# Hybrid state-space and linear-attention trunk: coefficient loads three tiles ahead, output-map signs on the powers, norm scale on the last projection's weights

## The chip, the cores and the metric

The kernel runs on one core of a Trainium2 chip. The metric is device microseconds of that core, the median of the timed runs shown. The profile is of one further execution, taken by the hardware profiler.

## The reference

Two layers act on one sequence of 512 positions with 1024 channels, all in float32. Each layer is `x <- x + RMSNorm(mixer(RMSNorm(x)))`. Cut to what matters here:

```python
def s5_layer(u, lam_re, lam_im, log_dt, b_re, b_im, c_re, c_im, d):
    lam = lax.complex(lam_re, lam_im)
    lam_bar = jnp.exp(lam * jnp.exp(log_dt)[:, None])
    b_bar = ((lam_bar - 1.0) / lam)[..., None] * lax.complex(b_re, b_im)
    bu = jnp.einsum('gnp,blgp->blgn', b_bar, u)
    _, states = lax.associative_scan(combine, (a, bu), axis=1)   # s_t = lam_bar s_{t-1} + bu_t
    y = jnp.einsum('gpn,blgn->blgp', lax.complex(c_re, c_im), states).real
    return y + d * u

def gla_branch(p, w_gate_up, b_gate, norm_g):
    q, k, v, r, lr = jnp.split(p, ...)
    g = jax.nn.log_sigmoid(lr @ w_gate_up + b_gate) / 16
    o = gla_chunked(heads(q) * 256 ** -0.5, heads(k), heads(v), heads(g))   # 4 heads, 64 positions a chunk
    return rms_norm(o, norm_g).reshape(1, 512, 2048) * jax.nn.silu(r)

# layer 0: p = u @ ev_w_in; ya = gelu(s5_layer(a_in)); ya = ya * sigmoid(ya @ w_glu + b) * silu(a_z)
#          yb = conformer_conv(b_val, b_gate: causal depthwise convolution, 31 taps) * silu(b_z)
#          y = concat([ya, yb]) @ ev_w_out
# layer 1: y = gla_branch(u @ od_w_in, ...) @ od_w_out
```

The state-space layer has 64 groups of 16 channels, each with a complex state of 64. The scale `norm_g` of the head norm in layer 1 has 512 entries, the same for each of the 4 heads.

## The kernel before, in words

**Projections.** A float32 product is made of three TensorE products of rounded halves: high by high, high by low, low by high (`mm_st` L181, `mm_mv` L792). All weights come in one list of 0.5 MB blocks of 128 x 1024 in the order of use. `w_raw` (L113) issues a block's load on SyncE's queue into one of three buffers `wraw` (L118). `w_split` (L134) makes the high half `wh` by a ScalarE cast (L143, two buffers) and the low half `wl` (three buffers): for blocks 0 to 47 and 56 to 63 by a negated ScalarE copy (L130) and an accumulating DMA that GpSimd issues (L131), for the others by a VectorE subtraction (L149). A few blocks, the last four of the list among them, go into buffers of their own (`wres`, `hres`, `lres`).

**State space.** The channels are worked in eight tiles of 128 (c = 0 to 7). `s5_params` (L308) computes the powers of the state's factor, `pr` (real and imaginary, 64 groups x 9 powers) and `prb` (the powers times the input map). `s5_prep(c)` (L513) loads tile c's coefficients `cb` (256 KB: both parts of the output map, both parts of the input map; L519, two buffers), and ScalarE makes two signed copies: `csp` (real part, sign by partition half, L522, which is also the stationary side of a matmul at L551) and `ci` (minus the imaginary part, L523, one buffer). For each half of the tile's groups an outer product of `prb` and the input map gives `bmt` (L528, L530, L532, on VectorE for c = 0 and 1, on GpSimd after), TensorE transposes it (L544), ScalarE copies that to `bm` (L546); TensorE multiplies `csp` by `bmt` (L551), ScalarE copies the result out to `ks` (L554), TensorE transposes `ks` (L555) and VectorE adds it into `kt` (L557). An outer product of `pr` with `csp` and `ci` on VectorE gives `cme` (lines L528, L530 and L532 again, the product with `ci` in the tile `pt`). GpSimd makes phase tables `ph` (L507 to L509) for each pair of tiles, which SyncE copies to `ct` and `st` (L573).

**Convolution.** h (L680) is a gated product, followed by 31 multiply-adds a tile on VectorE (L655), low in priority.

**Linear attention.** `gate(h)` (L965) takes the projection of head h, ScalarE applies SiLU (L970), and GpSimd multiplies by the norm scale, broadcast to all partitions in `ng` (L939, 128 x 512): L971, four times a head. VectorE scales the head's attention output by its inverse root mean square and this gate (L1129). The result is split into `oth` and `otl` and multiplied by the blocks of `w_out1`: eight for heads 0 and 1, in the course of head 2, and eight for heads 2 and 3 at the end, in `proj_tail` (L872; matmuls L800 to L802 and, for the last four blocks, L894 to L898).

**What sets the order.** The Tile framework orders each engine's instructions by simulating a timeline (`schedule_with_timeline_sim=True`), with priorities: `feed()` raises, `background()` lowers. Each engine then runs its own list strictly in order, and a waiting instruction holds everything behind it on that engine. DMAs stand in the list of the engine that issues them, mostly SyncE.

Of the kernel before, what the change touches and what calls it, by code (L numbers as in the profile page):

```python
# [9 lines left out]
F32 = mybir.dt.float32  # L10
F32R = mybir.dt.float32r
# [6 lines left out]
P = 128  # L18
# [33 lines left out]
def trunk(ctx: ExitStack, tc: tile.TileContext, A: dict, out: bass.AP, dbg: dict | None = None):  # L52
# [50 lines left out]
    for h in range(HEADS):  # L103
        wv, wr = ([A["w_vr"][o + h, j] for j in range(4)] for o in (0, 4))
        wqk = [A["w_qk"][2 * h + j] for j in range(2)] + [A["w_qk"][8 + 2 * h + j] for j in range(2)]
        wlist.extend(wv + wr + wqk if h == 0 else wqk + wv + wr)
        if h >= 2:
            for n in range(2):
                for j in range(4):
                    wlist.append(A["w_out1"][n, (h - 2) * 4 + j])  # L110
    wst = {"next_raw": 0, "next_split": 0, "raw": {}, "hl": {}, "low": {}}

    def w_raw():  # L113
        i = wst["next_raw"]
        if i >= len(wlist):
            return
        raw = wpool.tile([P, 1024], F32, tag="wraw", bufs=3, name=f"wraw{i}")
        SY.dma_start(raw, wlist[i])  # L118
        wst["raw"][i] = raw
        wst["next_raw"] = i + 1  # L120
# [13 lines left out]
    def w_split(dst=None):  # L134
# [6 lines left out]
        h = wpool.tile([P, 1024], F32R, tag="wh", bufs=2, name=f"wh{i}") if dst is None else dst[0]  # L141
        with feed():
            SC.copy(h, raw)  # L143
# [12 lines left out]
    def feed():  # L156
        return tc.high_priority(offset=1500)
# [150 lines left out]
    def s5_params():  # L308
# [148 lines left out]

        G.memset(md, 0.0)
# [53 lines left out]

    def s5_prep(c):  # L513
# [4 lines left out]
        cb = h5.tile([P, 4, GC, GP], F32, tag="cb", bufs=2, name=f"cb{c}")  # L518
        SY.dma_start(cb, A["s5cb"][c])  # L519
        cr_ = csps[c % 2]  # L520
        ci_ = h5.tile([P, GC, GP], F32, tag="ci", bufs=1, name=f"ci{c}")
        SC.activation(cr_[:, :, 0:GP], cb[:, 0], AF.Copy, scale=sgn)  # L522
        SC.mul(ci_, cb[:, 1], -1.0)  # L523
# [13 lines left out]
        for h in range(2):  # L537
# [22 lines left out]
            outer(V, cme[:, hs], pt2, h, pr, cr_[:, hs, 0:GP], ci_[:, hs], 3)  # L560
            yield
        kd = kt_d[c % 2]
# [136 lines left out]

    for c in range(2):  # L700
        run(s5_prep(c), 5)
# [236 lines left out]
    ng = pa.tile([P, S], F32, name="ng")  # L938
    SY.dma_start(ng, A["gla_g"].partition_broadcast(P))  # L939
# [25 lines left out]
    def gate(h):  # L965
        accs = proj_mv(u1h, u1l)
        rg = []
        for tt in range(TT):
            r_ = sbt_((P, S), F32, f"rg{h}{tt}")
            SC.activation(r_, accs[tt], AF.Silu)  # L970
            G.tensor_tensor(out=r_, in0=r_, in1=ng, op=ALU.mult)  # L971
            rg.append(r_)
        return rg
# [247 lines left out]
```

## Time and profile before

| | |
|---|---|
| Timed runs | 941.74, 946.74, 941.3 us; median 941.74 |
| Profiled execution, its own time | 946.76 us |
| its span (first to last instruction) | 945.0 us |
| mean granted TensorE clock | 0.983 |
| TensorE matmuls busy | 899.4 us (95%) |
| VectorE busy | 640.9 us (68%) |
| ScalarE busy | 482.6 us (51%) |
| GpSimd busy | 249.1 us (26%) |

The profiled execution took 1.76 us beyond its span. In rows of a timeline the first number is the start in us from the span's start, the second the duration in us, then engine, line and operation, the output tile, `<-`, the inputs and the shapes. In brackets at the end is how long the engine had been idle before, and what released it. SPq is SyncE's queue: a row there is the issue of a DMA, not its transfer, and its duration with xN includes the waits between N issues. Line numbers are those of the kernel before.

### The profile page before, as it was taken

What the parts mean: (1) busy time and instruction counts of PE and PEld (TensorE: products, weight loads), DVE (VectorE), ACT (ScalarE), POOL (GpSimd) and SP (SyncE); (2) the same over time, 40 slices, a digit from 0 to 9 for tenths busy, and PEclk for the clock granted to TensorE, in tenths of its full rate; (3) what the DMA queues carried; (4) which work ended last, traced back from release to release, by engine and by line L of the source; (5) the groups of instructions that cost most, each with busy time, mean ns of one, the idle gap of its engine ahead of it and who ended that gap; (6) DMA issues with size and microseconds to landing.
All of it is one profiled execution on the core that took longest, in us unless ns stands there. A gap on an engine that the chain in (4) does not pass through costs nothing.

```text
span 945.0 us, 12129 instructions
## 1 busy us (share of the span) xinstructions
PE 899.4 (95%) x4396; PEld 720.8 (76%) x4396; DVE 640.9 (68%) x1206; ACT 482.6 (51%) x691; POOL 249.1 (26%) x258
## 2 busy tenths in 40 slices
PE   5995998999999999999998979999999999999996
PEld 4873776777777887778887768888888888888875
DVE  7952999999989989832568546695384232744646
ACT  6542785876678855564444555343543242523430
POOL 2793656563123422011045002010200020000222
PEclk9998999999999999999999989999999999999998
DMA  9978887788988885289454112202222224324412
GB/s 272 252 184 203 222 203 183 179 194 204 216 219 229 205 235 183 86 223 204 154 193 139 49 58 98 84 29 90 89 76 80 75 82 136 133 89 164 192 45 89
DMA packets 54955, 142.74 MB, mean 151 GB/s; under 512 B 14256, under 2 KB 15792, under 8 KB 54896
## 3 DMA queue, kind: packets, MB, share of 16 engines
q1 hardware_dynamic: 46832, 112.62, 36.0%
q0 software_dynamic: 8064, 29.36, 17.2%
q8 instruction: 34, 0.56, 0.2%
q14 instruction: 25, 0.20, 0.1%
HBM read 95.18 MB, written 13.22 MB: 115 GB/s over the span
## 4 chain that ended last, share of the span: by engine, by line
PE 69%; DVE 12%; ACT 3%; DMA 3%; issue 1%; POOL 0%; DVEq 0%; ACTq 0%
PE ps_mm L186 10%; PE ps_mm L187 10%; PE ps_mm L189 10%; PE ps_mm L802 10%; PE ps_mm L800 9%; PE ps_mm L801 9%; DVE ps_cv L655 3%; PE ps_aux L1082 2%; DMA wraw<-in_w_vr_dram 1%; PE ps_aux L628 1%; DVE cme L528 1%; DVE pt L530 1%; DMA wraw<-in_w_out_dram 1%; PE ps_mm L894 1%; PE ps_mm L895 1%
## 5 line engine op out<-in xcount | busy, mean ns | idle before, releaser
L143 ACT CAST wh<-wraw 128x1024 fp32r<-128x1024 f32 x126 | 132.0, 1048 | 160.9 <-PE ps_mm L801 93.2
L149 DVE TENSOR_TENSOR wl<-wraw,wh 128x1024 fp32r<-128x1024 f32 x70 | 86.7, 1240 | 123.0 <-ACT wh L143 123.0
L655 DVE SCALAR_TENSOR_TENSOR ps_cv<-h,cw,ps_cv 128x512 f32<-128x512 f32 x232 | 161.8, 747 | 2.7 <-ACT ps_cv L652 1.8
L186 PE MATMUL ps_mm<-u0h,wh 128*128 128x512 f32 x320 | 128.5, 403 | 0.4 <-DVE u0l L305 0.2
L187 PE MATMUL ps_mm<-u0l,wh 128*128 128x512 f32 x320 | 128.1, 401 | 0.0
L800 PE MATMUL ps_mm<-wh,u1h 128*128 128x512 f32 x240 | 95.9, 401 | 3.5 <-ACT wh L143 3.1
L801 PE MATMUL ps_mm<-wh,u1l 128*128 128x512 f32 x240 | 96.1, 400 | 0.0
L131 POOL DMA_DIRECT2D wl<-wraw x56 | 48.9, 883 | 178.4 <-ACT wl L130 172.6
L802 PE MATMUL ps_mm<-wl,u1h 128*128 128x512 f32 x240 | 93.0, 404 | 1.7 <-DVE wl L149 1.7
L189 PE MATMUL ps_mm<-u0h,wl 128*128 128x512 f32 x320 | 82.7, 396 | 0.9 <-DMA wl<-wraw 0.9
L130 ACT ACTIVATE wl<-wraw 128x1024 fp32r<-128x1024 f32 x56 | 59.2, 1057 | 27.0 <-DMA wraw<-in_w_in_dram 14.0
L186 PEld LDWEIGHTS ps_mm<-u0h,wh 128*128 128x128 f32 x320 | 61.0, 191 | 15.3 <-issue 1.1
L187 PEld LDWEIGHTS ps_mm<-u0l,wh 128*128 128x128 f32 x320 | 61.0, 191 | 13.8 <-issue 1.1
L189 PEld LDWEIGHTS ps_mm<-u0h,wl 128*128 128x128 f32 x320 | 59.3, 188 | 15.1 <-DMA wl<-wraw 1.8
L800 PEld LDWEIGHTS ps_mm<-wh,u1h 128*128 128x128 f32 x240 | 45.8, 191 | 15.0 <-ACT wh L143 3.6
L971 POOL TENSOR_TENSOR rg<-rg,ng 128x512 f32<-128x512 f32 x16 | 24.2, 1542 | 123.6 <-ACT rg L970 123.6
L802 PEld LDWEIGHTS ps_mm<-wl,u1h 128*128 128x128 f32 x240 | 45.9, 192 | 13.3 <-DVE wl L149 2.5
L801 PEld LDWEIGHTS ps_mm<-wh,u1l 128*128 128x128 f32 x240 | 45.9, 191 | 10.6
L187 PE MATMUL ps_mm<-u1l,wh 128*128 128x512 f32 x128 | 50.3, 393 | 0.0
L186 PE MATMUL ps_mm<-u1h,wh 128*128 128x512 f32 x128 | 50.2, 392 | 0.0
L1065 POOL TENSOR_TENSOR kr<-kr,fac 128x384 f32<-128x384 f32 x8 | 9.1, 1133 | 124.5 <-DVE rr L205 65.1
L800 PE MATMUL ps_mm<-wh,oth 128*128 128x512 f32 x96 | 37.8, 396 | 0.6 <-ACT wh L143 0.6
(341 smaller groups left out, 2001.5 us busy)
## 6 DMA issues: line engine op xcount, KB each, us to landing
wl<-wraw POOLq DMA_DIRECT2D x56, 512.0 KB, 5.9
wraw<-in_w_in_dram SPq DMA_DIRECT2D x40, 512.0 KB, 4.9
wraw<-in_w_out_dram SPq DMA_DIRECT2D x32, 512.0 KB, 3.2
wraw<-in_w_vr_dram SPq DMA_DIRECT2D x32, 512.0 KB, 3.2
wraw<-in_w_qk_dram SPq DMA_DIRECT2D x16, 512.0 KB, 3.2
tm<-kt_d SPq DMA_DIRECT2D x8, 512.0 KB, 6.2
wraw<-in_w_glu_dram SPq DMA_DIRECT2D x8, 512.0 KB, 5.6
wraw<-in_w_pw_dram SPq DMA_DIRECT2D x8, 512.0 KB, 4.5
```

What stands on the lines that cost most here:

```text
L130: SC.activation(l, raw, AF.Copy, scale=-1.0)
L131: G.dma_start(l.bitcast(F32), raw, accum_op=ALU.add)
L143: SC.copy(h, raw)
L149: V.tensor_tensor(out=l, in0=raw, in1=h.bitcast(F32), op=ALU.subtract)
L186: PE.matmul(acc, whv[:, k, :], xh[:, k, :], start=(k == 0), stop=False)
L187: PE.matmul(acc, whv[:, k, :], xl[:, k, :], start=False, stop=False)
L189: PE.matmul(acc, wlv[:, k, :], xh[:, k, :], start=False, stop=(k == KT - 1))
L655: V.scalar_tensor_tensor(out=acc, in0=h[:, k:k + S], scalar=cw[:, c, k:k + 1], in1=acc, op0=ALU.mult, op1=ALU.add)
L800: PE.matmul(accs[tt], xh[:, kt, ts_], whj, start=(first and j == 0), stop=False)
L801: PE.matmul(accs[tt], xl[:, kt, ts_], whj, start=False, stop=False)
L802: PE.matmul(accs[tt], xh[:, kt, ts_], wlj, start=False, stop=(last and j == 1))
L971: G.tensor_tensor(out=r_, in0=r_, in1=ng, op=ALU.mult)
```

## The change

Three edits. First, the coefficient tile `cb` gets three buffers, tiles 0 to 2 are loaded before the preparation starts, and tile c + 3 is loaded at the end of tile c's preparation. Second, after `prb` is made, the signs go once onto the powers: `pr`'s real part is multiplied by the sign column, its imaginary part by −1, two VectorE operations of 128 x 576. The outer products for `cme` read `cb` directly, `ci` and its eight ScalarE copies are gone; `csp` stays for the matmul. Third, the norm scale is no longer multiplied into the gates. It is loaded as 4 x 128, transposed on TensorE to a column tile `ngc` of 128 x 4, and applied to the 16 blocks of `w_out1` in `w_split`: the block is worked in two halves of 512 columns, each a ScalarE activation with the scale (high) and a VectorE scalar_tensor_tensor (scale and subtract, low).

```diff
@@ -107,7 +107,7 @@
         if h >= 2:
             for n in range(2):
                 for j in range(4):
-                    wlist.append(A["w_out1"][n, (h - 2) * 4 + j])
+                    wlist.append((j % 2, A["w_out1"][n, (h - 2) * 4 + j]))
     wst = {"next_raw": 0, "next_split": 0, "raw": {}, "hl": {}, "low": {}}
 
     def w_raw():
@@ -115,7 +115,7 @@
         if i >= len(wlist):
             return
         raw = wpool.tile([P, 1024], F32, tag="wraw", bufs=3, name=f"wraw{i}")
-        SY.dma_start(raw, wlist[i])
+        SY.dma_start(raw, wlist[i][1] if isinstance(wlist[i], tuple) else wlist[i])
         wst["raw"][i] = raw
         wst["next_raw"] = i + 1
 
@@ -139,6 +139,18 @@
             w_low(i, dst and dst[1])
         raw = wst["raw"].pop(i)
         h = wpool.tile([P, 1024], F32R, tag="wh", bufs=2, name=f"wh{i}") if dst is None else dst[0]
+        if isinstance(wlist[i], tuple):
+
+            l = wpool.tile([P, 1024], F32R, tag="wl", bufs=3, name=f"wl{i}") if dst is None else dst[1]
+            for e in range(2):
+                es_, g_ = slice(e * S, (e + 1) * S), wst["gain"][:, 2 * wlist[i][0] + e:2 * wlist[i][0] + e + 1]
+                with feed():
+                    SC.activation(h[:, es_], raw[:, es_], AF.Copy, scale=g_)
+                    V.scalar_tensor_tensor(out=l[:, es_], in0=raw[:, es_], scalar=g_, in1=h[:, es_].bitcast(F32), op0=ALU.mult, op1=ALU.subtract)
+            wst["hl"][i] = (h, l)
+            wst["next_split"] = i + 1
+            w_raw()
+            return
         with feed():
             SC.copy(h, raw)
         if i in dma_low:
@@ -455,6 +467,9 @@
             V.tensor_tensor(out=pt, in0=pr[:, 1, :, 1:9], in1=bc(f1), op=ALU.mult)
             V.tensor_tensor(out=prb[:, o], in0=prb[:, o], in1=pt, op=op)
 
+        V.tensor_scalar(out=pr[:, 0], in0=pr[:, 0], scalar1=sgn, scalar2=None, op0=ALU.mult)
+        V.tensor_scalar(out=pr[:, 1], in0=pr[:, 1], scalar1=-1.0, scalar2=None, op0=ALU.mult)
+
         G.memset(md, 0.0)
         G.affine_select(out=md, in_=md, pattern=[[-TB, GP]], compare_op=ALU.not_equal, fill=1.0, base=1 - TB, channel_multiplier=1)
         G.tensor_tensor(out=dg, in0=md.unsqueeze(1).to_broadcast([P, NG, GP]), in1=dd.unsqueeze(2).to_broadcast([P, NG, GP]), op=ALU.mult)
@@ -510,17 +525,22 @@
             out_.append(r_.rearrange("p g a b -> p (g a b)"))
         pair[c // 2] = out_
 
+    cbs = {}
+
+    def coefficients(c):
+
+        if c < KT:
+            cbs[c] = h5.tile([P, 4, GC, GP], F32, tag="cb", bufs=3, name=f"cb{c}")
+            SY.dma_start(cbs[c], A["s5cb"][c])
+
     def s5_prep(c):
 
         g0_ = c * GC
         pe_ = V if c < DVE_PREP else G
         gs = slice(g0_, g0_ + GC)
-        cb = h5.tile([P, 4, GC, GP], F32, tag="cb", bufs=2, name=f"cb{c}")
-        SY.dma_start(cb, A["s5cb"][c])
+        cb = cbs.pop(c)
         cr_ = csps[c % 2]
-        ci_ = h5.tile([P, GC, GP], F32, tag="ci", bufs=1, name=f"ci{c}")
         SC.activation(cr_[:, :, 0:GP], cb[:, 0], AF.Copy, scale=sgn)
-        SC.mul(ci_, cb[:, 1], -1.0)
 
         def outer(eng, o, pt, h, pw, m1, m2, pa):
             sh = list(o.shape)
@@ -557,8 +577,9 @@
                 V.tensor_tensor(out=kt[:, hs, :], in0=kp[:, P:2 * P].rearrange("p (g q) -> p g q", q=32)[:, :, 0:GP],
                                 in1=dg[:, g0_ + h * 4:g0_ + h * 4 + 4, :], op=ALU.add)
             pt2 = q5.tile([P, 4, TB, GP], F32, tag="pt", bufs=1, name=f"pt2_{c}")
-            outer(V, cme[:, hs], pt2, h, pr, cr_[:, hs, 0:GP], ci_[:, hs], 3)
+            outer(V, cme[:, hs], pt2, h, pr, cb[:, 0, hs], cb[:, 1, hs], 3)
             yield
+        coefficients(c + 3)
         kd = kt_d[c % 2]
         SY.dma_start(kd[:, 0:TB], kt.rearrange("p g q -> p (g q)"))
         tm = q5.tile([P, TB, GC, GP], F32, tag="tm", bufs=2, name=f"tm{c}")
@@ -697,6 +718,8 @@
         for _ in range(n):
             next(g)
 
+    for c in range(3):
+        coefficients(c)
     for c in range(2):
         run(s5_prep(c), 5)
     run(s5_in(0), 2)
@@ -935,8 +958,13 @@
     vh = pa.tile([P, TT, S], F32R, name="vh")
     vl = pa.tile([P, TT, S], F32R, name="vl")
     bcum = pa.tile([P, KT, S], F32, name="bcum")
-    ng = pa.tile([P, S], F32, name="ng")
-    SY.dma_start(ng, A["gla_g"].partition_broadcast(P))
+
+    ngr = pa.tile([TT, P], F32, name="ngr")
+    SY.dma_start(ngr, A["gla_g"].rearrange("(k p) -> k p", p=P))
+    wst["gain"] = pa.tile([P, TT], F32, name="ngc")
+    ngp = ps("cv")
+    PE.transpose(ngp[:, 0:TT], ngr, ident[0:TT, 0:TT])
+    V.tensor_copy(wst["gain"], ngp[:, 0:TT])
     reset = pa.tile([P, S], mybir.dt.bfloat16, name="reset")
     G.memset(reset, 1.0)
     G.memset(reset.rearrange("p (c t) -> p c t", t=64)[:, :, 0:1], 0.0)
@@ -968,7 +996,6 @@
         for tt in range(TT):
             r_ = sbt_((P, S), F32, f"rg{h}{tt}")
             SC.activation(r_, accs[tt], AF.Silu)
-            G.tensor_tensor(out=r_, in0=r_, in1=ng, op=ALU.mult)
             rg.append(r_)
         return rg
```

ScalarE's order near the wait of the state-space preparation, before (cb_1265 and ci_1267 are tile 3's coefficients and sign copy; wraw_1083 is weight block 11, ks_869 the copy for tile 1):

```order
51 L546 COPY bm_850<-ps_aux 128x512
52 L130 ACTIVATE wl_1117<-wraw_1083 128x1024
53 L523 ACTIVATE ci_1267<-cb_1265 128x128
54 L143 CAST wh_1182<-wraw_1083 128x1024
55 L554 COPY ks_869<-ps_aux 128x128
56 L546 COPY bm_850<-ps_aux 128x512
57 L679 ACT_TABLE_LOAD
58 L679 ACTIVATE tmp<-ps_mm 128x512
```

And after (wraw_1085 is block 11, ks_871 the same copy; the old lines L143, L546, L554 and L679 are now L155, L566, L574 and L700):

```order
48 L566 COPY bm_852<-ps_aux 128x512
49 L130 ACTIVATE wl_1119<-wraw_1085 128x1024
50 L155 CAST wh_1184<-wraw_1085 128x1024
51 L574 COPY ks_871<-ps_aux 128x128
52 L566 COPY bm_852<-ps_aux 128x512
53 L700 ACT_TABLE_LOAD
54 L700 ACTIVATE tmp<-ps_mm 128x512
```

The sign copy between wl and wh is gone, the rest stands as it did.

SyncE's order of DMAs at the same place, before (cb_1265 is tile 3's load):

```order
38 L573 DMA st_905<-ph_0_834 64x512 x2
39 L666 DMA u_d_447<-tmp 128x512
40 L118 DMA wraw_1083<-in_w_in_dram 128x1024
41 L118 DMA wraw_1115<-in_w_in_dram 128x1024
42 L118 DMA wraw_1184<-in_w_in_dram 128x1024
43 L519 DMA cb_1265<-in_s5cb_dram 128x512
```

And after, from a place further ahead (cb_830 is tile 3's load, cb_903 tile 4's; L534 is the coefficients' load, L594 the copies of ph, L687 the old L666):

```order
30 L118 DMA wraw_688<-in_w_in_dram 128x1024
31 L534 DMA cb_830<-in_s5cb_dram 128x512
32 L118 DMA wraw_723<-in_w_in_dram 128x1024
...
39 L594 DMA st_908<-ph_0_840 64x512 x2
40 L687 DMA u_d_449<-tmp 128x512
41 L118 DMA wraw_1085<-in_w_in_dram 128x1024
42 L118 DMA wraw_1117<-in_w_in_dram 128x1024
43 L118 DMA wraw_1186<-in_w_in_dram 128x1024
44 L534 DMA cb_903<-in_s5cb_dram 128x512
```

Tile 3's load now stands ten rows ahead of the block that it stood behind by three, and tile 4's stands where tile 3's was.

VectorE's order around the input map of tile 1, before (pt_2 and cme_962 are the output map of tile 2, pt_3 of tile 3; bmt and pt_1 the input map of tile 1):

```order
160 L530 TENSOR_TENSOR pt_2_984<-pr,ci_958 128x512
161 L530 TENSOR_TENSOR pt_1_854<-prb,cb_845 128x512
162 L528 TENSOR_TENSOR bmt_853<-prb,cb_845 128x512
163 L532 TENSOR_TENSOR bmt_853<-bmt_853,pt_1_854 128x512
164 L530 TENSOR_TENSOR pt_1_878<-prb,cb_845 128x512
165 L557 TENSOR_TENSOR kt_777<-ps_aux,dg 128x64
166 L528 TENSOR_TENSOR bmt_877<-prb,cb_845 128x512
167 L528 TENSOR_TENSOR cme_962<-pr,csp_454 128x512 x2
```

And after (L548, L550 and L552 are the old L528, L530 and L532; the two products for cme_962 stand eleven rows further ahead still):

```order
165 L550 TENSOR_TENSOR pt_2_984<-pr,cb_776 128x512
166 L552 TENSOR_TENSOR cme_962<-cme_962,pt_2_984 128x512
167 L550 TENSOR_TENSOR pt_2_1048<-pr,cb_776 128x512
168 L552 TENSOR_TENSOR cme_962<-cme_962,pt_2_1048 128x512
169 L550 TENSOR_TENSOR pt_3_1291<-pr,cb_830 128x512
170 L550 TENSOR_TENSOR pt_1_856<-prb,cb_774 128x512
171 L548 TENSOR_TENSOR bmt_855<-prb,cb_774 128x512
```

The output map of tile 2 and the first product of tile 3's now stand ahead of the input map of tile 1.

## The prediction

> **What bounds the kernel now.** I read first the busy time of each engine by stretches of the span, to see where TensorE isn't full; then the list of TensorE's waits; then the timeline around the longest of them, engine by engine, back to what began it. Columns of the first view: the stretch, its length, then busy us (and instructions) of TensorE's matmuls, of its weight loads, of VectorE, ScalarE and GpSimd, then the granted clock, the DMA share and GB/s.
>
> ```profile
> 71.00:94.00 23.00, 12.66 (x68) 8.83 (x68) 6.48 (x11) 5.64 (x10) 8.82 (x8) 0.83 0.80 200
> 94.00:118.00 24.00, 24.00 (x142) 18.47 (x142) 22.34 (x31) 17.09 (x25) 15.45 (x14) 0.95 0.87 224
> 142.00:165.00 23.00, 18.70 (x127) 14.28 (x127) 22.82 (x29) 12.78 (x20) 16.05 (x12) 0.93 0.76 184
> 700.00:800.00 100.00, 100.00 (x456) 81.79 (x455) 35.96 (x47) 33.49 (x47) 8.99 (x7) 1.00 0.28 95
> ```
>
> Late in the program TensorE has no free time and the others have more than half of theirs. Early it is otherwise: from 71 to 94 no engine is full, and from 142 to 165 VectorE is (22.82 of 23) while TensorE waits. The waits of TensorE, in all, times, longest:
>
> ```profile
> PE ps_aux L555 <- ACT ks L554: 10.3, 1, 10.3
> ```
>
> One wait of 10.3 us stands alone in the middle of the program. Its surroundings on TensorE (start, duration, then in brackets the idle time before it), with a shorter wait behind:
>
> ```profile
> 81.25 0.41 PE L551 MATMUL ps_aux<-bmt,csp 128*32 128x128 f32 x4
> 92.00 0.48 PE L555 MATMUL ps_aux<-ident,ks 128*128 128x128 f32 x1 [10.34 <-ACT ks L554]
> ...
> 94.43 0.63 PE L186 MATMUL ps_mm<-u0h,wh 128*128 128x512 f32 x1
> 94.85 0.63 PE L187 MATMUL ps_mm<-u0l,wh 128*128 128x512 f32 x1
> ...
> 97.35 0.40 PE L187 MATMUL ps_mm<-u0l,wh 128*128 128x512 f32 x1
> ...
> 150.23 1.09 PE L588 MATMUL ps_aux<-bm,u 128*64 128x128 f32 x16 [1.68 <-DMA u<-u_d]
> ...
> 151.60 0.40 PE L187 MATMUL ps_mm<-u0l,wh 128*128 128x512 f32 x1
> 151.83 0.40 PE L186 MATMUL ps_mm<-u0h,wh 128*128 128x512 f32 x1
> ```
>
> After the long wait the matmuls start 0.42 us apart (94.43 to 94.85); after the wait of 1.68 they start 0.23 apart. The stretch to 94 has a granted clock of 0.83. So the long wait also leaves TensorE at about half speed behind it. Why ks, a copy of 0.26 us, is late shows on ScalarE:
>
> ```profile
> 80.56 1.06 ACT L130 ACTIVATE wl<-wraw 128x1024 fp32r<-128x1024 f32 x1 [8.04 <-DMA wraw<-in_w_in_dram]
> 90.54 0.31 ACT L523 ACTIVATE ci<-cb 128x128 f32<-128x128 f32 x1 [8.92 <-DMA cb<-in_s5cb_dram]
> 90.75 1.03 ACT L143 CAST wh<-wraw 128x1024 fp32r<-128x1024 f32 x1
> 91.69 0.26 ACT L554 COPY ks<-ps_aux 128x128 f32<-128x128 f32 x1
> ```
>
> ks stands third behind a sign copy of channel tile 3 (ci), whose coefficients had not landed. SyncE shows why:
>
> ```profile
> 75.00 9.88 SPq L118 DMA_DIRECT2D wraw<-in_w_in_dram  x3
> 84.97 0.97 SPq L519 DMA_DIRECT2D cb<-in_s5cb_dram  x1
> ```
>
> The load of cb stood behind three weight loads that filled the queue for 9.88 us; 5.57 us after its issue at 84.97 ci starts. VectorE hangs on the same knot, twice:
>
> ```profile
> 68.44 0.69 DVE L530 TENSOR_TENSOR pt<-prb,cb 128x512 f32<-128x512 f32 x1 [9.14 <-POOL ph L509]
> ...
> 90.88 0.69 DVE L530 TENSOR_TENSOR pt<-pr,ci 128x512 f32<-128x512 f32 x1 [13.98 <-ACT ci L523]
> 94.38 0.69 DVE L680 TENSOR_TENSOR h<-ps_mm,tmp 128x512 f32<-128x512 f32 x1 [2.80 <-ACT tmp L679]
> ```
>
> h (L680) starts the convolution work, which fills VectorE from there on (22.34 of 24, later 22.82 of 23). So the start of h, not TensorE's clock, sets when this first part ends.
>
> **Change, part one: coefficients ahead, no ci.** The eight sign copies go, and tile 3's load moves ahead of weight loads that now stand before it; its new condition, VectorE being done with tile 0's output map, is met early. Then ScalarE meets wl at 80.56 as before, and behind it wh, ks, bm, the table load and tmp with no gap. From wh to ks it is 91.69 − 90.75 = 0.94; wl, of the same length, I give 0.95. So wh starts at 81.51 and ks at 82.45: 9.24 earlier than 91.69. bm, the table load, tmp and h follow at the distances that they have now, so h starts at 94.38 − 9.24 = 85.14. TensorE resumes at 92.00 − 9.24 = 82.76; its wait shrinks from 10.34 to 1.1, below the 1.68 that left the pitch at 0.23. Next late after ks is then wl at 80.56, which waits for its weight block, not for coefficients.
>
> TensorE gains more than that: between 92.0 and 97.35 it ran at about half speed (0.42 against 0.23; at 97.35 an entry is 0.40 long again), worth about half of 5.3 = 2.6. That part I count at nothing: from 142 to 165 TensorE waits for VectorE anyway (18.70 busy of 23). VectorE's start of h gains 9.24, and that is the term.
>
> Against it stands what VectorE now does earlier. With cb there, the output maps of tile 2 and half of tile 3 go ahead of its wait of 9.14 at 59 to 68: six 128x512 operations of 0.69 = 4.1 us, plus two sign multiplications on the powers before them. For those:
>
> ```profile
> L297 DVE TENSOR_SCALAR x<-x,rr 128x512 f32<-128x512 f32 x4 | 1.9, 482 | 0.0
> ```
>
> 128x576 by this row is 0.54 each, 1.1 us together. 4.1 + 1.1 = 5.2 fits in the 9.14, which covers it; without that cover it would be 5.2 on VectorE. But GpSimd makes ph in the same time, and it runs slower beside VectorE:
>
> ```profile
> 58.34 0.96 DVE L530 TENSOR_TENSOR pt<-pr,ci 128x512 f32<-128x512 f32 x1
> ```
> ```profile
> 56.58 1.10 POOL L401 TENSOR_TENSOR wb<-ya 128x64 f32<-128x64 f32 x1
> 60.27 0.41 POOL L401 TENSOR_TENSOR wb<-ya 128x96 f32<-128x96 f32 x1
> ...
> 67.13 1.28 POOL L509 TENSOR_TENSOR ph<-ph,wt 128x512 f32<-128x512 f32 x1
> ```
>
> While VectorE worked (until 58.34 + 0.96 = 59.30) the smaller operation took 1.10, after it the larger took 0.41. So each of the six may cost GpSimd between nothing and 1.10 − 0.41 = 0.7, in sum 0 to 4.1. ph matters: SyncE issues its copies, then the weight block for which wl waits at 80.56.
>
> ```profile
> 69.33 4.95 SPq L573 DMA_DIRECT2D st<-ph  x4
> ```
>
> The last ph ends at 68.41, the four copies run to 74.28, the weight loads begin at 75.00. A ph that is late by x moves wl, ks and h by x. I take x = 1, nearer the free end, since the first of the six meet GpSimd's small operations and weight-copy issues rather than ph. Part one is then −9.24 + 1 = −8.2, between −9.24 (or −11.8 with the clock) and −5.1.
>
> A rule bears on x. The Trainium skill, "SBUF — State Buffer", section "SBUF: two separate sides", says that a VectorE operation with two SBUF inputs and a GpSimd operation that reads SBUF exclude each other from a shared port pair, for a whole instruction each. The rows 1.10 and 0.41 agree in direction; by that rule alone each of the six would hold GpSimd for its whole length, which comes to about the −5.1. As a mechanism of this kernel it is a rival below.
>
> **Part two: norm scale on the last projection's weights.** Prices:
>
> ```profile
> L971 POOL TENSOR_TENSOR rg<-rg,ng 128x512 f32<-128x512 f32 x16 | 24.2, 1542 | 123.6 <-ACT rg L970 123.6
> L143 ACT CAST wh<-wraw 128x1024 fp32r<-128x1024 f32 x126 | 132.0, 1048 | 160.9 <-PE ps_mm L801 93.2
> L230 ACT ACTIVATE xg<-xg,rr 128x512 f32<-128x512 f32 x4 | 2.9, 724 | 8.8 <-DVE rr L205 5.0 <-DVE rs_t L202 2.2 <-POOL tmp L949 1.6
> L149 DVE TENSOR_TENSOR wl<-wraw,wh 128x1024 fp32r<-128x1024 f32 x70 | 86.7, 1240 | 123.0 <-ACT wh L143 123.0
> L1129 DVE SCALAR_TENSOR_TENSOR tmp<-ps_aux,rr,rg 128x512 f32<-128x512 f32 x16 | 12.0, 750 | 4.4 <-POOL rg L971 3.4
> ```
>
> GpSimd loses 24.2 us. For 16 blocks ScalarE pays 2 × 0.724 − 1.048 = 0.40 each, 6.4 in all; VectorE 2 × 0.750 − 1.240 = 0.26 each, 4.2 in all. Between 700 and 800 TensorE is full while VectorE has 64 and ScalarE 66.5 of 100 free: that hides it; uncovered, it would be 10.6. The halves also chain: the first low half can start after 0.72 rather than 1.05, so both are ready after 0.72 + 1.50 = 2.22, against 1.05 + 1.24 = 2.29. Only near the end is there less cover:
>
> ```profile
> 883.15 0.75 DVE L1129 SCALAR_TENSOR_TENSOR tmp<-ps_aux,rr,rg 128x512 f32<-128x512 f32 x1 [3.43 <-POOL rg L971]
> 904.77 0.50 PE L800 MATMUL ps_mm<-wh,oth 128*128 128x512 f32 x1 [0.57 <-ACT wh L143]
> ```
>
> Before 904.77 two ScalarE splits follow each other: +0.8. On the other side the GpSimd multiplication that held VectorE for 3.43 at 883 is gone, and with it this lag of the following splits; at most the wait of 0.57 goes. Between −0.6 and +0.8, I take 0. The column form of the scale needs a small transpose on TensorE near 520, and its load takes the place of a larger one; a wait there lies between 0 and, by the wait of 1.68 that a small load caused at 150.23, 1.7. I take 0, since its load is issued where the larger one was, and other matmuls stand before the transpose.
>
> **Sum.** −8.2 + 0 + 0 = −8.2. The profiled execution has this span (the first number):
>
> ```profile
> core 0: 945.0 us, clock 0.983
> ```
>
> Its own time is 946.76, so after it is 938.5. It lies 5.0 above the median of 941.74, with one of the three runs. Nothing shows where these 5 us lie; I take the gain as equal in both, so the median goes to 933.5.
>
> **Rivals.** *More* (chance 0.17): the clock's 2.6 counts as well, with x = 0: −11.8, 930. For it: TensorE is full from 94 to 118 (24.00), so it may be the bound there. Against: 142 to 165.
>
> *The stall moves* (0.27): ph comes later by 4.1, at 0.7 for each of the six operations, or the runs at 941 had the long wait only half as long. The first gives −5.1, 936.6; the second 9.24 − 5 = 4.2, 937.5. With both nearly nothing is left, 941. For it: 1.10 against 0.41. Then TensorE's leftover wait would be 3 to 5 us and the clock would drop again.
>
> *The coefficients block SyncE* (0.07), the slower one. The load for tile c + 3 waits until VectorE is done with tile c's output map, and weight loads stand behind it on SyncE. For tile 7:
>
> ```profile
> 148.58 0.33 SPq L118 DMA_DIRECT2D wraw<-in_w_in_dram  x1
> ...
> 161.82 0.54 SPq L118 DMA_DIRECT2D wraw<-in_w_in_dram  x1
> ```
> ```profile
> 152.86 2.04 DVE L530 TENSOR_TENSOR pt<-pr,ci 128x512 f32<-128x512 f32 x1
> ```
> ```profile
> SPq L519 <- POOL bmt L528: 14.4, 3, 8.1
> ```
>
> It would be reached after 148.58 and could go at 154.9, when tile 4's last product ends; the next weight load went at 161.82, so the slack is 6.9. It decides when VectorE falls behind SyncE by more than that. Such waits were up to 8.1 already; two of them uncovered, after tiles 3 and 4, plus the restart at half clock (2.6 each), are 21.4, less 8.2: +13, 955.
>
> *The early loads don't help* (0.04): the copies of ph still set 80.56 and something else holds ks; 941.7.
>
> **Chances.** The forecast (−7 to −10) has 0.45. About 1% (9.4 us) is what a measurement of this kernel can tell. Below 932.3 lie the first rival and the third of the forecast with x near 0, 0.17 + 0.16 and a little for what I don't see: 0.36. Above 951.2 lies the slower rival: 0.06 of its 0.07. The rest, 0.58, is within. The range runs from 928 (the full gain and the tail's 0.6, with some 1.5 of spread) to 942 (the stall moved whole).
>
> **What would show it.** After the change: no ci on ScalarE; cb of tile 3 issued before 65; ks within 2.5 us of its matmuls near 82; TensorE's wait at that place near 1.1 with a pitch of 0.23 behind it; h at 85 to 86 instead of 94.38; the convolution stretch as dense as now. If h is earlier by 9 and the end by less than 5, the bound between 94 and 220 was not VectorE. If L971's absence shows, VectorE's wait of 3.43 at 883 is gone. The prediction is wrong if the wait on ks stays above 4, or if SyncE's coefficient loads show waits above 7 with TensorE idle behind them.

## The result and the profile after

The changed kernel takes 935.31 us (median of 7 runs, 931.29 to 938.98); the kernel before, with runs on the same chips added, 944.34 (7 runs, 941.3 to 947.41). The ratio is 0.9906, with a 95% interval of 0.9885 to 0.9926. The forecast was 933.5, in a range of 928 to 942. The profiled execution took 936.94 us, 9.82 less than the profiled one before, with a span of 935.2.

The longest waits of TensorE after the start (in all, times, longest):

```profile
PE ps_mm L201 <- DMA wl<-wraw: 4.2, 3, 2.0
PE ps_mm L823 <- ACT wh L155: 3.1, 1, 3.1
PE ps_aux L609 <- DMA u<-u_d: 2.6, 2, 2.4
PE ps_aux L571 <- DVE kt L577: 2.1, 2, 1.4
PE ps_aux L575 <- ACT ks L574: 1.8, 1, 1.8
```

The wait on ks has gone from 10.3 to 1.8, the least of these five. Behind it the matmuls start 0.23 apart, where before they started 0.42 apart:

```profile
87.25 0.40 PE L199 MATMUL ps_mm<-u0l,wh 128*128 128x512 f32 x1
87.48 0.40 PE L198 MATMUL ps_mm<-u0h,wh 128*128 128x512 f32 x1
```

On ScalarE, and on VectorE for the first convolution product h (L701 is the old L680; start, duration, idle before):

```profile
82.84 1.06 ACT L130 ACTIVATE wl<-wraw 128x1024 fp32r<-128x1024 f32 x1 [9.08 <-DMA wraw<-in_w_in_dram]
83.80 1.03 ACT L155 CAST wh<-wraw 128x1024 fp32r<-128x1024 f32 x1
84.73 0.26 ACT L574 COPY ks<-ps_aux 128x128 f32<-128x128 f32 x1
```
```profile
87.42 0.69 DVE L701 TENSOR_TENSOR h<-ps_mm,tmp 128x512 f32<-128x512 f32 x1 [9.29 <-ACT tmp L700]
```

wl, wh and ks follow each other without ci between them. But wl itself starts at 82.84 rather than 80.56, so ks comes at 84.73 and h at 87.42: 6.96 earlier than 94.38, where the forecast had 8.2. What made wl late stands on VectorE, GpSimd and SyncE:

```profile
60.69 1.44 DVE L552 TENSOR_TENSOR cme<-cme,pt 128x512 f32<-128x512 f32 x1
62.17 1.45 DVE L550 TENSOR_TENSOR pt<-pr,cb 128x512 f32<-128x512 f32 x1
63.65 1.44 DVE L552 TENSOR_TENSOR cme<-cme,pt 128x512 f32<-128x512 f32 x1
```
```profile
60.07 3.00 POOL L522 TENSOR_TENSOR ph<-wb 128x512 f32<-128x512 f32 x2
63.03 1.52 POOL L523 TENSOR_TENSOR wt<-wb 128x512 f32<-128x512 f32 x1
...
68.27 1.61 POOL L524 TENSOR_TENSOR ph<-ph,wt 128x512 f32<-128x512 f32 x1
```
```profile
75.83 5.98 SPq L118 DMA_DIRECT2D wraw<-in_w_in_dram  x3
```

Of before, the same operations of GpSimd (the old L507 and L508) without VectorE beside them:

```profile
60.64 2.10 POOL L507 TENSOR_TENSOR ph<-wb 128x512 f32<-128x512 f32 x2
62.69 1.07 POOL L508 TENSOR_TENSOR wt<-wb 128x512 f32<-128x512 f32 x1
```

Side by side, each of the first three of GpSimd's operations costs about 0.45 more (1.52 for 1.07), the three behind them up to 0.34, and each of VectorE's about 0.75 more (1.44 for 0.69). The last phase table ends at 69.88 instead of 68.41 (+1.47), the weight loads begin at 75.83 instead of 75.00 (+0.83), and from there to wl it is 7.0 instead of 5.6. So the larger part of the 2.28 by which wl is late arises behind the issue of the load.

Three marks divide every profile of this study: the start of the last of the eight h products, the last table load of ScalarE (in the gate of head 3), and the end of the span.

| us | to the last h | from there to the table load | from there to the end | span |
|---|---|---|---|---|
| before | 316.8 | 561.7 | 66.5 | 945.0 |
| after | 306.9 | 563.8 | 64.5 | 935.2 |
| difference | −9.9 | +2.1 | −2.0 | −9.8 |

The middle is 558.6 to 563.8 in the thirteen profiles of the two kernels and of the experiments, in no order that follows the edits (both ends of it are kernels with the norm scale moved); much of the spread between executions may lie there. The first and the last stretch carry the change. The last is steady: 66.5 to 66.9 in the four kernels with the norm scale on the gates, 64.5 to 65.1 in the nine with it on the weights. The first is not: four kernels with the same coefficient edits that differ only in the norm scale or its place (the changed one and three of the experiments) have the last h at 306.6, 306.9, 308.0 and 311.1, so the 9.9 is one draw among 5.7 to 10.2.

### The profile page after: what moved, and what is told of

It reads as the page before. It is cut to its first block, busy times and chain, and to the rows that moved or that the text cites. A ratio compares the mean times of both kernels' runs of the same rounds, so it can differ in the third digit from the quotient of the medians.

```text
span 935.2 us, 12132 instructions
## 1 busy us (share of the span) xinstructions
PE 895.1 (96%) x4397; PEld 718.9 (77%) x4397; DVE 645.2 (69%) x1225; ACT 485.1 (52%) x699; POOL 225.0 (24%) x242
## 5 line engine op out<-in xcount | busy, mean ns | idle before, releaser
L155 ACT CAST wh<-wraw 128x1024 fp32r<-128x1024 f32 x114 | 119.5, 1049 | 138.5 <-PE ps_mm L824 61.9
L161 DVE TENSOR_TENSOR wl<-wraw,wh 128x1024 fp32r<-128x1024 f32 x58 | 71.6, 1235 | 85.7 <-ACT wh L155 85.7
L149 DVE SCALAR_TENSOR_TENSOR wl<-wraw,ngc,wh 128x512 fp32r<-128x512 f32 x24 | 17.0, 747 | 39.3 <-ACT wh L148 39.3
L903 POOL TENSOR_TENSOR yp<-yp,gain 128x512 f32<-128x512 f32 x8 | 12.6, 1591 | 118.9 <-ACT junk L230 118.9
```

The lines of the kernel that those rows point to most:

```text
L161: V.tensor_tensor(out=l, in0=raw, in1=h.bitcast(F32), op=ALU.subtract)
```

## The experiments

The theory at the start: the wait for tile 3's coefficients carries the gain; it is worth what h moves; the early output maps cost part of it; the move of the norm scale is worth little.

**The edits one by one.** First all but the norm scale's move; the diff is against the changed kernel.

```diff
-                    wlist.append((j % 2, A["w_out1"][n, (h - 2) * 4 + j]))
+                    wlist.append(A["w_out1"][n, (h - 2) * 4 + j])
...
+            G.tensor_tensor(out=r_, in0=r_, in1=ng, op=ALU.mult)
```

> The coefficient and sign edits alone; the norm scale stays a GpSimd multiplication of the gates. Theory (the coefficient wait carries the gain): the first convolution product h starts near 87.4 us as in the changed kernel, and the time is within 2 us of the changed kernel, so 7 to 9 us under the kernel before. Rival (the end of the program, 1.65 us shorter in the changed kernel's profile, is owed to the norm scale's move and counts): only 5 to 7 us under, and VectorE waits 3.4 us for the GpSimd multiplication near the end again.

Measured: 937.18 us, ratio to the kernel before 0.9916 (0.9895 to 0.9937). Its profiled execution had ks and h late (wl at 85.68, h at 90.27, where 87.4 was expected), and the last stretch at 66.9. The theory held for the size, 7.5 by the medians. The 1.9 that separates it from the changed kernel is the norm scale's by the theory, but the two intervals overlap. Then the norm scale alone; this diff and the next two are against the kernel before.

```diff
-            G.tensor_tensor(out=r_, in0=r_, in1=ng, op=ALU.mult)
...
+                    SC.activation(h[:, es_], raw[:, es_], AF.Copy, scale=g_)
+                    V.scalar_tensor_tensor(out=l[:, es_], in0=raw[:, es_], scalar=g_, in1=h[:, es_].bitcast(F32), op0=ALU.mult, op1=ALU.subtract)
```

> The norm scale on the last projection's weights alone; coefficients and signs as before. Theory: the wait of 10.3 us on ks stays, the time is 0 to 1.7 us under the kernel before. Rival (the longer splits cost): 1 to 3 us over, with TensorE waits on weights between 735 and 905 us.

Measured: 942.72, ratio 0.9981 (0.9965 to 0.9998), 1.8 us under by the ratio. The wait on ks stays at 8.5. The end of the program is 64.5 long, as in the changed kernel. So the third edit is a gain of its own, small and only just clear of its interval, but seen in the last stretch of every profile; the rival falls.

Next, the loads ahead with ci kept.

```diff
-        cb = h5.tile([P, 4, GC, GP], F32, tag="cb", bufs=2, name=f"cb{c}")
-        SY.dma_start(cb, A["s5cb"][c])
+        cb = cbs.pop(c)
...
+        coefficients(c + 3)
```

> The loads three tiles ahead alone: ScalarE still makes ci, so VectorE's output maps of tile 2 cannot go early (the zero tile is halved and written in two DMAs each, to make room for the third buffer). Theory (what held ScalarE was the landing of the coefficients, and the early output maps delay the phase tables by 1.5 us): ks and h as in the changed kernel or up to 2 us earlier, h at 85 to 87.5, time 7 to 11 us under the kernel before. Rival (the sign copy in ScalarE's queue is itself the cause): ks late by more than 4 us, time less than 4 us under.

Measured: 936.9, ratio 0.9911 (0.9896 to 0.9926). Its ScalarE and GpSimd:

```profile
81.42 1.06 ACT L130 ACTIVATE wl<-wraw 128x1024 fp32r<-128x1024 f32 x1 [7.35 <-DMA wraw<-in_w_in_dram]
82.39 0.29 ACT L531 ACTIVATE ci<-cb 128x128 f32<-128x128 f32 x1
82.59 1.03 ACT L143 CAST wh<-wraw 128x1024 fp32r<-128x1024 f32 x1
83.53 0.26 ACT L562 COPY ks<-ps_aux 128x128 f32<-128x128 f32 x1
```
```profile
63.14 1.07 POOL L509 TENSOR_TENSOR wt<-wb 128x512 f32<-128x512 f32 x1
...
66.38 1.07 POOL L509 TENSOR_TENSOR wt<-wb 128x512 f32<-128x512 f32 x1
67.52 1.29 POOL L510 TENSOR_TENSOR ph<-ph,wt 128x512 f32<-128x512 f32 x1
```

ci stands where it stood before and costs 0.2 us, since its coefficients are there. The rival, that the copy in the queue was the cause, falls: the landing was. Without early output maps GpSimd runs at 1.07, and h comes at 86.21. The time is that of the changed kernel and, within the intervals, the norm scale's 1.8.

Last, the signs alone: no ci, but two buffers and tile 3's load behind the weight loads.

```diff
-        ci_ = h5.tile([P, GC, GP], F32, tag="ci", bufs=1, name=f"ci{c}")
...
-        SC.mul(ci_, cb[:, 1], -1.0)
...
-            outer(V, cme[:, hs], pt2, h, pr, cr_[:, hs, 0:GP], ci_[:, hs], 3)
+            outer(V, cme[:, hs], pt2, h, pr, cb[:, 0, hs], cb[:, 1, hs], 3)
```

> The signs on the powers alone, two coefficient buffers, tile 3's load where it was. ScalarE has no ci to wait for, so ks is free as in the changed kernel (TensorE's wait on it 1 to 3 us); but VectorE's product with tile 3's coefficients stands ahead of h and waits for their landing near 90. Theory (VectorE's start of h sets the end of the first part): h at 90 to 92.5, time 2 to 4.5 us under the kernel before. Rival (TensorE's wait sets it): the time is 7 to 10 us under, as in the changed kernel.

Measured: 944.59, ratio 0.9982 (0.9961 to 1.0003): 0.1 us under by the medians, 1.7 by the ratio, nothing that is clear of the interval. The expected 2 to 4.5 us did not come. VectorE and TensorE's waits in it:

```profile
92.62 0.69 DVE L531 TENSOR_TENSOR pt<-pr,cb 128x512 f32<-128x512 f32 x1 [16.40 <-DMA cb<-in_s5cb_dram]
93.37 0.68 DVE L681 TENSOR_TENSOR h<-ps_mm,tmp 128x512 f32<-128x512 f32 x1
```
```profile
PE ps_aux L552 <- DVE kt L558: 9.5, 3, 8.4
```

The wait moved over to VectorE. Its product with tile 3's coefficients stands at the head of the queue for 16.4 us, and behind it kt, for which TensorE now waits 8.4 us. So the run didn't separate VectorE's start of h from TensorE's wait, as it was meant to: both were late. What it shows is that taking the operation out of one in-order queue is worth little or nothing while another in-order queue waits for the same load.

**The cost of the early output maps.** In the next run tile 2's map waits for the phase tables (diffs from here on are against the changed kernel).

```diff
             pt2 = q5.tile([P, 4, TB, GP], F32, tag="pt", bufs=1, name=f"pt2_{c}")
+            if c == 2:
+                G.tensor_copy(out=cme[:, h * 4, 0, 0:1], in_=pair[0][1][:, 0:1])
+                if h == 0:
+                    G.tensor_copy(out=pt2[:, 0, 0, 0:1], in_=pair[0][1][:, 0:1])
```

> The changed kernel, with tile 2's output map made to wait for the phase tables (GpSimd copies one column of the last table into the tiles that the map writes, so VectorE's six early operations come after it). Theory (the early VectorE operations beside GpSimd's phase tables cost x = 1.5 us): GpSimd's large operations there take 1.07 rather than 1.5 us, the last table ends near 68 instead of 69.9, and h comes 1 to 2.5 us earlier than 87.4 if the map still fits ahead of h; time 0 to 2 us under the changed kernel. Rival (GpSimd's tables do not set when the weight block lands): tables earlier, h where it was.

Measured: 933.47, ratio 0.9889 (0.9871 to 0.9906), 1.8 us under the changed kernel by the medians, though the two intervals overlap.

```profile
63.29 1.07 POOL L523 TENSOR_TENSOR wt<-wb 128x512 f32<-128x512 f32 x1
...
67.70 1.29 POOL L524 TENSOR_TENSOR ph<-ph,wt 128x512 f32<-128x512 f32 x1
```
```profile
86.30 0.69 DVE L705 TENSOR_TENSOR h<-ps_mm,tmp 128x512 f32<-128x512 f32 x1 [6.19 <-ACT tmp L704]
```

GpSimd is back at 1.07, the tables end at 68.99, 0.9 earlier, and h comes 1.1 earlier. But the link between the two is not the expected one:

```profile
76.24 9.78 SPq L118 DMA_DIRECT2D wraw<-in_w_in_dram  x3
```
```profile
81.71 1.06 ACT L130 ACTIVATE wl<-wraw 128x1024 fp32r<-128x1024 f32 x1 [5.97 <-DMA wraw<-in_w_in_dram]
```

The weight load is issued 0.4 later than in the changed kernel, and wl still starts 1.1 earlier, because 5.5 us pass between the two and not 7.0. The other profiles sort the same way. From the issue to wl it is 5.2 to 5.6 in the three kernels whose output map of tile 2 waits until the tables are done (before, the norm scale alone, the loads ahead with ci), 5.7 in the signs alone, where it is worked beside half of them, and 6.8 to 8.2 in the six in which it is worked beside the tables. So the theory held for GpSimd and for h, but the early maps cost more by a slower landing of the weight block than by a later issue; why it lands later was not tested. The opposite dose, six more products in the same stretch:

```diff
+            if c == 2:
+                for _ in range(3):
+                    V.tensor_tensor(out=pt2, in0=pr[:, 1, g0_ + h * 4:g0_ + h * 4 + 4, 0:TB].unsqueeze(3).to_broadcast([P, 4, TB, GP]),
+                                    in1=cb[:, 1, hs].unsqueeze(2).to_broadcast([P, 4, TB, GP]), op=ALU.mult)
```

> The changed kernel with six more 128x512 VectorE products of two SBUF inputs for tile 2, written over and not used, in the stretch beside GpSimd's phase tables. Theory: GpSimd's remaining large operations stay at 1.4 to 1.6 us, the tables end up to 0.5 us later than 69.9, VectorE reaches the input map of tile 1 about 6 x 1.1 = 6 us later than 70.4, and its idle 9.3 us before h takes this up only in part, since tile 1's chain to ks lies behind it on VectorE: ks and h later by 3 to 6 us, time 3 to 6 us over the changed kernel. Rival (the idle time before h hides all of it): no difference.

Measured: 935.84, ratio 0.9917 (0.9901 to 0.9934): 0.5 us over the changed kernel by the medians, not 3 to 6.

```profile
PE ps_aux L564 <- DVE bmt L552: 5.8, 1, 5.8
```
```profile
88.30 0.69 DVE L705 TENSOR_TENSOR h<-ps_mm,tmp 128x512 f32<-128x512 f32 x1 [3.24 <-ACT tmp L704]
```

VectorE was late with the input map of tile 1, and TensorE waited 5.8 us for it. But wl still could not start before its weight block landed (83.14 in this run), so ks and h moved by only 0.5 and 0.9: the expectation had left that second wait out. TensorE did lose time: of the 5.8 it saved 2.2 in waits on ks that the changed kernel has, and the last h stands at 310.59 in this profile, 3.7 behind. The medians show 0.5 of that; the middle stretch of this profile is 2.7 shorter than the changed kernel's, which the edit does not touch. So the size stays open.

**Which engine sets the first stretch.** VectorE got 12 us less to do there: 8 of the 31 convolution taps are left out for two tiles.

```diff
-        for k in range(1, 30):
+        for k in range(9 if c < 2 else 1, 30):
```

> The changed kernel with 8 of the 31 convolution taps left out for channel tiles 0 and 1: 16 VectorE operations of 0.75 us, 12 us less on VectorE between 89 and 165. Theory (VectorE sets the pace from h to 210, where TensorE has 122.9 - 116.1 = 6.7 us of idle time to lose): 4 to 7 us under the changed kernel. Rival (TensorE's own work sets it): less than 1.5 us under.

Measured: 934.77, ratio 0.9905 (0.9878 to 0.9932), 0.5 under the changed kernel. Busy time in one and the same stretch (columns as in the first view of the prediction), in the changed kernel and then with fewer taps:

```profile
94.00:210.00 116.00, 109.56 (x719) 84.43 (x717) 114.86 (x159) 83.58 (x119) 68.59 (x57) 0.99 0.84 207
```
```profile
94.00:210.00 116.00, 107.16 (x719) 82.33 (x718) 114.41 (x153) 84.03 (x119) 69.66 (x57) 1.00 0.87 217
```

VectorE is as full as before, 114.4 of 116: the freed time was taken by convolution work of later tiles, which has low priority and waits in line. And the end hardly moved. In the profile the last h came 1.6 us earlier, no more than separates kernels that are alike up to there. So VectorE's fullness was mostly a backlog being worked off, not the bound, and the theory that VectorE sets the pace from h on falls: it asked for 4 to 7 us.

**Where the norm scale's gain comes from.** Unused space was put where the broadcast scale had been: 1504 bytes a partition, so that what is allocated behind it stands in its old place.

```diff
+    pad = pa.tile([P, 376], F32, name="pad")
+    G.memset(pad[:, 0:4], 0.0)
```

> The changed kernel with 1504 bytes a partition of unused space where the broadcast scale stood, so that what is allocated behind it stands where it did before the change. Theory (the last four TensorE groups take 5.44 rather than 5.62 us for 24 matmuls because their operands lie elsewhere in SBUF): groups at 5.62 again, the end of the program 0.5 to 0.8 us later. Rival (it is owed to which engines write the weights, or to their values): groups stay at 5.44, no difference.

VectorE takes over the result of each of the last groups of 24 matmuls, so the distance of these rows is a group's length. Before, then after, then with the old place:

```profile
931.04 0.69 DVE L900 TENSOR_TENSOR yp<-ps_mm,yp 128x512 f32<-128x512 f32 x1 [0.51 <-PE ps_mm L898]
...
936.66 0.69 DVE L900 TENSOR_TENSOR yp<-ps_mm,yp 128x512 f32<-128x512 f32 x1 [0.49 <-PE ps_mm L898]
```
```profile
921.43 0.69 DVE L923 TENSOR_TENSOR yp<-ps_mm,yp 128x512 f32<-128x512 f32 x1 [0.31 <-PE ps_mm L921]
...
926.87 0.69 DVE L923 TENSOR_TENSOR yp<-ps_mm,yp 128x512 f32<-128x512 f32 x1 [0.32 <-PE ps_mm L921]
```
```profile
918.62 0.69 DVE L923 TENSOR_TENSOR yp<-ps_mm,yp 128x512 f32<-128x512 f32 x1 [0.50 <-PE ps_mm L921]
...
924.24 0.69 DVE L923 TENSOR_TENSOR yp<-ps_mm,yp 128x512 f32<-128x512 f32 x1 [0.50 <-PE ps_mm L921]
```

5.62, 5.44, and 5.62 again. The last stretch is 65.1 long in this run, 0.6 over the changed kernel's; 935.52 us in all, ratio 0.9919 (0.9895 to 0.9943), which is too coarse to tell 0.6. With 96 bytes, in one execution:

> The same with 96 unused bytes a partition. Small shift: if the pitch depends on the place within some hundred bytes, the last groups leave 5.44 us; if on coarser places, they stay.

```profile
912.66 0.69 DVE L923 TENSOR_TENSOR yp<-ps_mm,yp 128x512 f32<-128x512 f32 x1 [0.37 <-PE ps_mm L921]
918.25 0.69 DVE L923 TENSOR_TENSOR yp<-ps_mm,yp 128x512 f32<-128x512 f32 x1 [0.47 <-PE ps_mm L921]
```

5.59: a small shift already leaves 5.44. A shift of 2048 bytes, which would have told whether only the place within 2048 bytes counts, does not fit into SBUF, so that stays open. In the other profiles the group takes 5.62 wherever the norm scale is on the gates and 5.44 wherever it is on the weights without a shift. So 0.6 of the 2.0 at the end is owed to where operands lie in SBUF, and has nothing to do with the edit's arithmetic.

For the other 1.4, here is TensorE's way from the first attention matmul behind the gate of head 3 to the first matmul with an `hres` block, before and after:

```profile
883.05 0.39 PE L1119 MATMUL ps_aux<-vh,al 128*128 128x512 f32 x1
...
911.20 0.40 PE L894 MATMUL ps_mm<-hres,oth 128*128 128x512 f32 x1
```
```profile
874.95 0.39 PE L1146 MATMUL ps_aux<-vh,al 128*128 128x512 f32 x1
...
902.04 0.39 PE L917 MATMUL ps_mm<-hres,oth 128*128 128x512 f32 x1
```

That is 28.15 before and 27.09 after, 1.06 less. The wait of 0.57 on a ScalarE split (904.77 before) lies in it, with the delays right behind it, and is gone: all four profiles with the norm scale on the gates have a wait of 0.6 to 0.9 there, none of the nine others has one. The last 0.3 is the mark's own: the table load stands behind a split that takes 1.34 now and took 1.05 before. Which part of the edit removes the wait was not tried by itself; the last `hres` block is split 24.7 us after the table load, against 25.3 before, and GpSimd's multiplication, which had held VectorE there, is gone.

**Can the weight block come earlier?** Four of the eight copies ahead of it on SyncE went to GpSimd's queue; first in the changed kernel, then together with the later output map.

```diff
-                SY.dma_start(dst[r_ * NS:r_ * NS + NS], src[half])
+                (G if c < 2 and dst is st_ else SY).dma_start(dst[r_ * NS:r_ * NS + NS], src[half])
```

> The changed kernel, with the four copies of the second phase table of tiles 0 and 1 issued by GpSimd, which makes the table, instead of SyncE, so that the next weight block no longer stands behind them: its load goes at 70 to 71 rather than 75.8. ks and h then come up to 5 us earlier (h at 82 to 84), while TensorE has only its wait of 1.8 us at ks to gain there. Theory (the start of h sets the end of the first part): the last h and the end come 3 to 5 us earlier than in the changed kernel. Rival (TensorE's own row of matmuls sets it): 0 to 2 us earlier.

> Both moves: tile 2's output map after the phase tables, and the copies of the second table issued by GpSimd. If the two are independent, h is at 81 to 83.5 and the time 2 to 4 us under the changed kernel; if the loads or TensorE's row limit it, no better than the first of them alone, 1 to 2 us under.

Measured: 933.36, ratio 0.9887 (0.9859 to 0.9916), and 933.32, ratio 0.9888 (0.9857 to 0.9919). Both are about 2 us under the changed kernel by the medians, no better than the later map alone. In the second of them, SyncE, then ScalarE, then a window, and the same window in the changed kernel:

```profile
70.90 0.54 SPq L118 DMA_DIRECT2D wraw<-in_w_in_dram  x1
```
```profile
80.86 1.06 ACT L130 ACTIVATE wl<-wraw 128x1024 fp32r<-128x1024 f32 x1 [6.81 <-DMA wraw<-in_w_in_dram]
```
```profile
72.00:84.00 12.00, 11.40 (x66) 7.78 (x67) 7.52 (x13) 4.28 (x8) 6.12 (x10) 1.00 1.02 241
```
```profile
72.00:84.00 12.00, 10.88 (x59) 7.96 (x55) 3.45 (x6) 2.32 (x5) 4.41 (x4) 1.00 1.00 262
```

The block's load is issued 4.9 us earlier than in the changed kernel, but wl starts 10 us after it instead of 7: the DMA engines' share is at its top, 1.02 in this stretch and 1.00 in the changed kernel. By these rows the transfers are the limit here, and no longer the place in SyncE's queue; a run with less traffic was not made. That is where the forecast's chain (tables, SyncE, weight block, ks) now ends. Since h didn't come earlier in the first of them (87.84; the load was issued at 73.00, not at 70 to 71, since the tables ended late, and wl again came 10 us behind it), that run couldn't separate its two theories. In the second h was at 85.45, not at the 81 to 83.5 of independent moves. The three versions of 933.3 to 933.5 are the fastest of this study; none is clear of the changed kernel by its interval.

## Why the prediction was right, and where its steps were not

The time fell 9.0 us by the medians, for which −8.2 was forecast. Both the place and the main cause were right; of the terms several were off, and they nearly cancelled. That the sum came within 1 us is luck: in the profiles the first stretch gave 1.7 more than forecast and the last 2.0 more, and the middle, for which nothing was forecast, took 2.1 back.

- **Coefficients off ScalarE's path.** Right. The wait of 10.34 became 1.76 (forecast 1.1), wl, wh and ks follow without a gap, and the loads ahead alone give it all (936.9) while the signs alone give nothing that can be told from the spread (944.59). That the signs made room for the third buffer and freed the early maps is their part.
- **What the early maps cost (x = 1).** Right in that they cost, off in size and in part of the way. The tables were 1.47 late and wl 2.28. Of the 1.47 only 0.83 reached the issue of the weight load; the other 1.45 came behind it, on the load itself, where the forecast had left the distance from issue to wl as it was (5.6, now 7.0). And VectorE's operations were priced at 0.69 each, from rows where nothing ran beside them; the six that ran beside the tables took 1.44 to 2.14. The idle 9.14 that was to cover 5.2 is gone entirely. The lock of the Trainium skill ("SBUF — State Buffer", "SBUF: two separate sides") was too strong a rule for this case: if the two operations excluded each other for their whole lengths, a pair would take 0.69 + 1.07 = 1.76, and it took 1.44 to 1.52. It was near enough that it should have been applied to VectorE's price too, which the forecast did not do.
- **The clock counted at nothing.** By the changed kernel's profile this step failed. I argued that VectorE, full from 94 to 220, sets the end of the first part, so that only h counts (−6.96 as measured). The first stretch shortened by 9.9. TensorE's own account comes nearer: its wait at ks less by 8.6, the half-speed matmuls behind it by 2.6 (the forecast's estimate), and its other waits up to the last h longer by about 2 in sum, together about −9. The argument from 142 to 165 was also misread: of TensorE's 4.3 idle there, 1.68 was a wait for the load of u and only 1.93 one for VectorE. The run with fewer taps speaks for TensorE's account: VectorE stayed full, and little happened. So does the run with six more products, whose first h moved by 0.9 and whose last h moved by 3.7. TensorE's account is what the rival "More" had named as its mechanism; its size, 11.8, was spoilt by the 2.28 above. What the half speed itself is worth these runs don't settle: with the loads ahead and ci kept, the last h came 7.6 earlier for 8.2 of the first.
- **The norm scale at 0, between −0.6 and +0.8.** Wrong by its bounds: −2.0 in the last stretch of the profile, of which 0.3 is the mark's, and −1.8 by timing it alone. The prices were right (ScalarE's halves 0.716, VectorE's 0.747, against 0.724 and 0.750). The wait of 0.57 did go, but with the delays behind it that is 1.06, and the +0.8 that was set against it never reached TensorE. What I left out was the matmuls' pitch, 0.6, which no row of before could show.
- **The profiled run's 5 us over the median.** Taking the gain as equal in both was right: −9.8 between the profiles, −9.0 between the medians. With seven runs the times of the kernel before fill 941.3 to 947.4 evenly, and the middle stretch alone varies by 5 us. Their median is 2.6 above the 941.74 that the forecast started from; from 944.34 it would have said 936.1.
- **The slower rival.** SyncE's coefficient loads waited 11.2 us in two waits, the longest 6.0, within the slack of 6.9 that was given, and no wait of TensorE goes back to them.

```profile
SPq L534 <- DVE pt L550: 11.2, 2, 6.0
```

## What to carry to other kernels

When a wait ends on a load, ask which in-order queues hold an instruction that needs it: moving the instruction from one queue to the next moves the stall (TensorE's wait of 10.3 behind ScalarE became one of 8.4 behind VectorE), moving the load ends it. An engine that is full because low-priority work is waiting in line is not thereby the bound; give it less to do, or see whether its tail is a backlog, before pricing a change by its start. Price an operation that goes next to GpSimd's large operations by rows where both run, for both engines. And when a load is issued earlier, or more work is moved beside it, don't carry the distance from its issue to its use over from the kernel before: here it went from 5.6 to 7 and to 10 us.

## What was not expected of the hardware

The pitch of a 128x512 matmul depended on where operands lay in SBUF: a group of 24 took 5.44 us, with a shift of 96 bytes a partition 5.59 (one execution), of 1504 bytes 5.62. The granted clock was the same. Before, and then after, in windows that hold these groups (the number behind POOL's):

```profile
918.00:937.00 19.00, 18.63 (x80) 14.64 (x78) 12.90 (x35) 2.90 (x8) 5.18 (x4) 1.00 0.18 68
```
```profile
908.00:927.00 19.00, 18.83 (x83) 15.21 (x82) 12.98 (x35) 2.89 (x8) 5.17 (x4) 1.00 0.16 60
```

1.00 in both, with 80 and 83 matmul records in 19 us. Which operand it hangs on, and at which distances, stays open.

Two SBUF-reading operations side by side, one on VectorE and one on GpSimd, took 1.44 and 1.52 us where alone they take 0.69 and 1.07.
